# c loaded as eight rows and spread by TensorE, its columns behind x, Sqrt's table ahead of the squares

## The chip, the cores and the metric

The kernel runs on one core of a Trainium2 chip. The metric is the device time of one execution in microseconds, as the median of several runs of the same program. The engines of a core are TensorE (PE; its weight loads are listed as PEld), VectorE (DVE), ScalarE (ACT), GpSimd (POOL) and SyncE (SP), which here issues all DMAs. Each engine takes its instructions in the order in which they were written out, and waits for others by semaphores.

## The reference

One decoder block on x (1024 tokens by 1024 features, float32), steered by one vector c of 1024 numbers:

```python
c_act = silu(c)
cond = c_act @ ada_w + ada_b              # six vectors of 1024: shift1, scale1, gate1, shift2, scale2, gate2
h = rmsnorm(x, norm1_g) * (1 + scale1) + shift1
u, v, val, gate = split(h @ w_in + b_in, 4)
y_a = spatial_gating_mixer(gelu(u), gelu(v), ...)      # chunks of 128 tokens
y_b = conformer_conv_mixer(val, gate, ...)             # causal depthwise conv, width 31
x = x + gate1 * (concat(rmsnorm(y_a), rmsnorm(y_b)) @ w_out)
h2 = rmsnorm(x, norm2_g) * (1 + scale2) + shift2
g, up = split(h2 @ w_ffn_in, 2)
x = x + gate2 * ((silu(g) * up) @ w_ffn_out)
return rmsnorm(x, norm_f_g) * (1 + scale_f) + shift_f  # from c_act @ ada_f_w + ada_f_b
```

The change is about the first two lines and the first rmsnorm: how c and silu(c) reach the engines, and what stands in front of the first product `h @ w_in`.

## The kernel before, in words

**Layout.** Features lie on the 128 partitions, tokens along the free axis. x is held transposed in eight row blocks k of 128 features, and in two halves of 512 tokens, in tiles of two row blocks (`xs[half][i]`). A product in float32 is done as three products of rounded parts, hi x hi, lo x hi and hi x lo (`mm3`, lines 712 to 716; `product`, line 1142): ACT rounds a tile to its hi part, DVE or POOL subtracts to get the lo part.

**The front (lines 586 to 941).** SP issues, in a fixed turn (`in_turn`): the first x tile, c as one row on one partition, the early columns of `colt` (c, the ada biases and norm1's gain as columns), the other x tiles of the first half (the last one in two pieces), then the weights for row block 0: `ada1` (the scale's columns for block 0), one `ada` row block (for the shift) and the first `wk`, then the late columns. TensorE begins with ten matmuls on zeros (`WARM_UP`, line 872). Then it spreads c over all partitions: for each half of c one matmul of a single partition (K = 1) with 512 columns (line 624), and ACT takes Silu of each into `cact` (line 625). Silu of the columns of c is taken apart (line 620). Only then ACT loads the table for Sqrt (line 627).

The first rmsnorm (`first_rstd`, line 845) squares the eight row blocks, some on DVE (`BY_VECTOR`) and some on ACT, into five buffers, sums each over the partitions with four matmuls of 32 columns (line 858), puts matmuls on zeros between them (`IDLE`, `keep_busy`, line 839), takes the square root on ACT (line 862) and the reciprocal on DVE (line 863), and spreads the result over the partitions with matmuls (line 866). The scale of row block 0 comes from `ada1` by matmul (line 891) and a copy (line 894); the other scale and shift columns come from DVE, which multiplies a 128x1024 row block of `ada` by `cact` and sums along the row (line 665). Then per row block k: t = x times the rstd (909 for k = 0, 919 for the others), h = t times scale plus shift in its hi part (922, 924) and its lo part (932, 933), the hi and lo parts of `wk` (697, 698), and 24 matmuls into eight banks (lines 714 to 716).

**After the front.** The u product of the first half (`u_proj`, lo parts of its weights on POOL), the rstd of the second half, the v, value and gate products, the convolution's taps on DVE (line 1071), the mixers, the output projection, then the feed-forward in a Strassen-like form (`product`, line 1147) and the last norm.

**The order.** All engines' orders come from a planner. The program is first written down with its dependencies; `Graph` collects them, `forward` plays the program with a duration for each instruction (`duration`) and for each DMA (`LOAD_WAIT`, `LOAD_RATE`), `backward` gives each step the length of what follows it, and `fix_order` repeats the two `ROUNDS_OF_ORDER` times, with a small random number added to each rank from `SEED`. The order that results is fixed for the whole program on every engine. `in_turn`, `on["V"]` and `on["A"]` are chains that the planner must keep: the loads, DVE's and ACT's steps of the front. Tiles with the same tag share a few buffers (`rt` has two, `cv` and `gn` two PSUM banks each); a new tile waits for the last reader of the old one.

Of the kernel before, what the change touches and what calls it, by code (L numbers as in the profile page):

```python
# [7 lines left out]
F32 = mybir.dt.float32  # L8
F32R = mybir.dt.float32r
BF16 = mybir.dt.bfloat16  # L10
AF = mybir.ActivationFunctionType
ALU = mybir.AluOpType

P = 128
S = 1024
D = 1024
KD = D // P
# [12 lines left out]
N_RAW = 4  # L30
# [2 lines left out]
N_AHEAD = 12  # L33
N_FILL = 8
N_POOL_TAPS = (6, 6)
IDLE = (4, 6, 6, 6, 4)
WARM_UP = 10
BY_VECTOR = (1, 3, 4, 5, 7)
BEFORE_LAST = ((3, 6), (2, 4), (3, 7), (3, 2))
# [5 lines left out]
SHIFT1, SCALE1, GATE1, SHIFT2, SCALE2, GATE2, SHIFTF, SCALEF = range(8)  # L45

_COLS = [
    ("c", 8), ("ada_b", 64), ("norm1_g", 8), ("norm2_g", 8), ("norm_f_g", 8), ("b_in", 16),
    ("a_ln_g", 4), ("a_ln_b", 4), ("b_conv_b", 4), ("b_gn_g", 4), ("b_gn_b", 4),
    ("out_norm_a_g", 4), ("out_norm_b_g", 4), ("b_conv_w", 4 * CW),  # L50
    ("picks", 4), ("low_rows", 1), ("sel_hl", 1),
# [19 lines left out]
SIGNAL = {"PE": 0.043, "DVE": 0.024, "Activation": 0.024, "Pool": 0.068, "SP": 0.05}  # L71
TABLES = ("Sqrt", "Silu", "Sigmoid", "Gelu")
TABLE_LOAD = 1.295
LOAD_WAIT, STORE_WAIT, LOAD_RATE, STORE_RATE = 2.05, 1.29, 350e3, 376e3
LOAD_GAP, STORE_GAP, TURN_GAP = 0.07, 0.24, 0.3
DMA_ISSUE = 0.44
DMA_AHEAD = 0.5
SHORT_ROWS = 1.15
CLOCK_WINDOW = 3.4133
MARGIN = (1.03, 1.1)  # L80
ROUNDS_OF_ORDER, SPREAD, SEED = 4, 0.05, 577509


class Step:
# [452 lines left out]
def block_kernel(ctx: ExitStack, tc: tile.TileContext, xT, c, ada, ada1, cols, vbias, bs, wsp,  # L537
                 wv, wu, wk, wvg, wo, wf, wfo, wfl, cst, out):
    nc = tc.nc
    V, A, G, PE = nc.vector, nc.scalar, nc.gpsimd, nc.tensor  # L540
# [3 lines left out]
    @contextmanager  # L544
    def issue_after(ins):
        n = len(nc.cur_bb.bb.instructions)
        yield
        edges.extend((i.name, ins.name) for i in nc.cur_bb.bb.instructions[n:] if i.engine == ins.engine)

    const = ctx.enter_context(tc.tile_pool(name="const", bufs=1))  # L550
    sb = ctx.enter_context(tc.tile_pool(name="sb", bufs=1))
# [13 lines left out]
    def gn_bank(name):  # L565
        return ps.tile([P, 512], F32, tag="gn", name=name, bufs=2)
# [16 lines left out]
    def hs(half):  # L583
        return slice(half * H, (half + 1) * H)

    c_row = sb.tile([P, D], F32, tag="raw", name="c_row", bufs=N_RAW)
    colt = const.tile([P, NCOL], F32, name="colt")
    xs = [[const.tile([P, 2, H], F32, name=f"x{half}_{i}") for i in range(KD // 2)] for half in range(2)]
    early = _OFF["norm2_g"]
    in_turn = [nc.sync.dma_start(xs[0][0], xT[0, 0]).ins, nc.sync.dma_start(c_row[0:1, :], c).ins,  # L590
               nc.sync.dma_start(colt[:, 0:early], cols[:, 0:early]).ins]
    in_turn += [nc.sync.dma_start(xs[0][i], xT[0, i]).ins for i in range(1, KD // 2 - 1)]
    in_turn += [nc.sync.dma_start(xs[0][KD // 2 - 1][:, a, :], xT[0, KD // 2 - 1, :, a, :]).ins for a in range(2)]

    def x_tile(k, part):
        half = part.start // H
        return xs[half][k // 2][:, k % 2, part.start - half * H:part.stop - half * H]
# [8 lines left out]
    ones = const.tile([P, 1], F32, name="ones")  # L606
    V.memset(ones, 1.0)
    epst = const.tile([P, 1], F32, name="epst")
# [7 lines left out]
    warm = const.tile([P, 1], F32, name="warm")  # L616
    A.activation(warm, epst, AF.Silu)
    cact = const.tile([P, D], F32, name="cact")
    cact_cols = colt[:, 0:KD]
    A.activation(cact_cols, cact_cols, AF.Silu)  # L620
    silu, on = [], dict(V=[], A=[])
    for h in range(2):
        cb = cv_bank(f"c{h}")
        PE.matmul(cb, ones[0:1].broadcast_to([1, P]), c_row[0:1, hs(h)], start=True, stop=True)
        silu.append(A.activation(cact[:, hs(h)], cb, AF.Silu).ins)
    with issue_after(silu[-1]):
        A.activation(warm, epst, AF.Sqrt)


    cond = const.tile([P, 64], F32, name="cond")  # L630
# [214 lines left out]
    def first_rstd():  # L845

        bank = nrm_bank("ssq_n1_0")
        for k in range(KD):
            src = x_tile(k, hs(0))
            t = tmp(f"sq_n1_0_{k}")  # L850
            if k in BY_VECTOR:
                on["V"].append(V.tensor_tensor(t, src, src, op=ALU.mult).ins)
            else:
                on["A"].append(A.activation(t, src, AF.Square).ins)
                if k == 0:
                    on["A"] += silu
            for q in range(4):
                mm = PE.matmul(bank[q * 32:(q + 1) * 32, 0:P], ones.broadcast_to([P, 32]),
                               t[:, q * P:(q + 1) * P], start=k == 0, stop=k == KD - 1).ins
            keep_busy(IDLE[k // 2] if k % 2 else 0, mm)  # L860
        rt = sb.tile([P, P], F32, tag="rt", name="rt_n1_0", bufs=2)
        on["A"].append(A.activation(rt, bank[:, 0:P], AF.Sqrt, bias=epst, scale=1.0 / D).ins)
        last["rstd"] = V.reciprocal(rt, rt).ins
        on["V"].append(last["rstd"])
        for q in range(4):
            mm = PE.matmul(bank[:, q * P:(q + 1) * P], sel_tok[:, q:q + 1].broadcast_to([P, P]),
                           rt, start=True, stop=True).ins
        keep_busy(IDLE[4], mm)
        return bank
# [28 lines left out]
    for k in range(KD):  # L898
# [21 lines left out]
        h = h1[0][k] = act_tile(f"h1_0_{k}", 0)  # L920
# [349 lines left out]
    for p in range(4):  # L1270
        b11, b21, b12, b22 = (ev(f"h2_{n}_{p}") for n in ("11", "21", "12", "22"))
        for kh, (t0, t1) in enumerate(((b11, b12), (b21, b22))):
            k = p + 4 * kh
# [84 lines left out]
    for i, f in enumerate(order):  # L1358
        full7, st, b_bank, s1, up0 = started[f]
        c_bank = cv_bank(f"C_{f}")  # L1360
# [49 lines left out]
    eye = sb.tile([P, P], F32, tag="rt", name="eye", bufs=2)  # L1410
# [72 lines left out]
    for r, pairs in enumerate(ROUNDS):  # L1483
# [10 lines left out]
        base = 0 if last_round else 8 * r  # L1494
# [56 lines left out]
    with issue_after(last_ins):  # L1551
# [6 lines left out]
        for i in (1, 2):  # L1558
            part = pieces[i]
            cols = slice(part.start - H, part.stop - H)  # L1560
# [94 lines left out]
```

## Time and profile before

| | |
|---|---|
| runs | 962.04 us median of 3 (961.86 to 964.15) |
| profiled execution, from its first to its last instruction | 962.3 us |
| TensorE busy | 947.2 us, 98% |
| DVE busy | 859.0 us, 89% |
| ACT busy | 478.8 us, 50% |
| POOL busy | 411.0 us, 43% |
| first product of the front (line 714) | 18.89 us |
| first product of u (line 714, tile pu) | 63.84 us |

The span is the profiled execution's own time: 962.3 us, 0.26 above the median of the runs. In the rows of the timeline the first number is the start in us, the second the time in us, then engine, line, operation, output and inputs, shapes and count; the bracket names the idle time before it and what ended it. "ns" rows by source line give the least, the median and the longest duration, then the first and last start. In the windows view each engine has its busy time in the stretch and the number of instructions, then follow the granted clock of TensorE, the DMA share and GB/s. The chain of waits is followed back from the last instruction.

### The profile page before, as it was taken

The numbers are of one execution on the slowest core, as the hardware profiler recorded it, in microseconds if no ns is written. First come the engines' busy times: TensorE is split into PE (matmuls) and PEld (weight loads), VectorE is DVE, ScalarE is ACT, GpSimd is POOL, SyncE is SP. The second block draws the span as 40 slices with busy tenths as digits, with TensorE's granted clock in tenths as the row PEclk, the third lists the DMA queues.
The fourth block names the chain that finished last, engine by engine and source line by source line (L and its number), as shares of the span: only waits on it lengthen the run. The fifth ranks groups of instructions, "written<-read, shape, count | busy, mean of one in ns | idle before, by whom it ended". The sixth has DMA issues, their size and how long they took to land.

```text
span 962.3 us, 12994 instructions
## 1 busy us (share of the span) xinstructions
PE 947.2 (98%) x4505; PEld 769.7 (80%) x4505; DVE 859.0 (89%) x1234; ACT 478.8 (50%) x771; POOL 411.0 (43%) x253
## 2 busy tenths in 40 slices
PE   8999999999999999999999999999999999999996
PEld 5787787788778778788888888888888888888885
DVE  5978999999999973899999999999978889969956
ACT  4688468863473753564233233332237437227526
POOL 0059997876364313663545534545454200000132
PEclk9999999999999999999999999999999999999998
DMA  8875352353476354844676766667758747414104
GB/s 306 297 278 178 131 176 88 131 182 131 146 267 214 117 175 150 267 167 156 235 250 223 257 225 212 224 231 263 244 173 283 266 164 262 162 33 157 64 0 175
DMA packets 70931, 184.25 MB, mean 191 GB/s; under 512 B 8017, under 2 KB 8529, under 8 KB 70866
## 3 DMA queue, kind: packets, MB, share of 16 engines
q1 hardware_dynamic: 70866, 183.43, 55.1%
q8 instruction: 35, 0.57, 0.3%
q14 instruction: 30, 0.25, 0.1%
HBM read 142.24 MB, written 41.16 MB: 191 GB/s over the span
## 4 chain that ended last, share of the span: by engine, by line
PE 89%; DVE 5%; issue 2%; POOL 2%; ACT 1%; ACTq 0%; POOLq 0%; DVEq 0%
PE B L1147 32%; PE C L1147 18%; PE ah L1147 11%; PE A L1147 4%; PE po L714 3%; PE po L715 3%; PE po L716 3%; PE v L714 2%; PE v L715 2%; PE v L716 2%; PE p L714 1%; PE p L715 1%; PE pu L715 1%; PE p L716 1%; PE pu L716 1%
## 5 line engine op out<-in xcount | busy, mean ns | idle before, releaser
L1147 PE MATMUL B<-h,w_f 128*128 128x512 f32 x816 | 189.7, 389 | 0.0
L1147 PEld LDWEIGHTS B<-h,w_f 128*128 128x128 f32 x816 | 153.1, 188 | 32.1 <-ACT x L1366 0.3
L1071 DVE SCALAR_TENSOR_TENSOR cv<-ypad,colt,cv 128x512 f32<-128x512 f32 x216 | 147.5, 746 | 0.2
L1147 PE MATMUL B<-fa,w_d 128*128 128x512 f32 x528 | 125.1, 389 | 0.0
L1147 PE MATMUL C<-h,w_f 128*128 128x512 f32 x528 | 123.7, 389 | 0.0
L1147 PEld LDWEIGHTS C<-h,w_f 128*128 128x128 f32 x528 | 99.1, 188 | 20.8 <-ACT w_f L1139 0.3
L1147 PEld LDWEIGHTS B<-fa,w_d 128*128 128x128 f32 x528 | 99.1, 188 | 20.6
L1147 PE MATMUL ah<-h,wh_a 128*128 128x512 f32 x320 | 100.4, 391 | 0.5 <-ACT h L731 0.5
L1434 POOL TENSOR_TENSOR sq_nf<-sq_nf,sq_nf 128x512 f32<-128x512 f32 (+1 forms) x15 | 18.4, 1226 | 170.6 <-ACT sq_nf L1428 170.5
L1139 ACT ACTIVATE w_f<-raw_f 128x512 fp32r<-128x512 f32 x68 | 41.9, 628 | 89.9 <-PE C L1147 32.0
L1139 ACT ACTIVATE w_d<-raw_d 128x512 fp32r<-128x512 f32 (+1 forms) x72 | 41.6, 593 | 82.8 <-PE B L1147 30.9
L698 POOL TENSOR_TENSOR wl_a<-raw_a,wh_a 128x1024 fp32r<-128x1024 f32 x20 | 49.0, 2454 | 76.2 <-ACT wh_a L697 76.1
L1147 PEld LDWEIGHTS ah<-h,wh_a 128*128 128x128 f32 x320 | 59.9, 188 | 14.1 <-ACT h L731 0.9
L1140 DVE TENSOR_TENSOR w_f<-raw_f,w_f 128x512 fp32r<-128x512 f32 x68 | 68.3, 1018 | 1.8 <-ACT w_f L1139 1.8
L1147 PE MATMUL C<-fa,w_d 128*128 128x512 f32 (+1 forms) x291 | 64.2, 370 | 0.0
L1147 PE MATMUL ah<-h,wl_a 128*128 128x512 f32 x160 | 62.3, 390 | 0.0
L1394 POOL TENSOR_TENSOR x<-x,u 128x512 f32<-128x512 f32 x22 | 39.4, 1791 | 46.8 <-DVE u L1393 46.8
L1147 PEld LDWEIGHTS C<-fa,w_d 128*128 128x128 f32 x291 | 51.0, 188 | 9.2
L1508 DVE SCALAR_TENSOR_TENSOR x<-B,cond,x 128x512 f32<-128x512 f32 x48 | 35.9, 749 | 19.0 <-PE B L1147 18.2
L1140 DVE TENSOR_TENSOR fa<-a,fa 128x512 fp32r<-128x512 f32 x77 | 50.1, 689 | 2.4 <-ACT fa L1139 2.4
L1391 POOL TENSOR_TENSOR x<-x,up 128x512 f32<-128x512 f32 x20 | 30.9, 1544 | 42.3 <-ACT x L1390 42.2
L1140 DVE TENSOR_TENSOR w_d<-raw_d,w_d 128x512 fp32r<-128x512 f32 (+1 forms) x72 | 48.5, 685 | 0.1
(288 smaller groups left out, 2120.8 us busy)
## 6 DMA issues: line engine op xcount, KB each, us to landing
acts<-x SPq DMA_DIRECT2D x77, 256.0 KB, 2.9
a<-acts SPq DMA_DIRECT2D x77, 256.0 KB, 4.1
raw_f<-wf SPq DMA_DIRECT2D x32, 512.0 KB, 4.1
ada<-ada SPq DMA_DIRECT2D x24, 512.0 KB, 3.3
x<-ada SPq DMA_DIRECT2D x24, 512.0 KB, 4.0
raw_a<-wf SPq DMA_DIRECT2D x20, 512.0 KB, 3.4
ahead<-ahead SPq DMA_DIRECT2D x40, 256.0 KB, 2.4
ypad<-ada SPq DMA_DIRECT2D x16, 512.0 KB, 4.5
```

Source lines behind the costliest of these rows:

```text
L698: lo_eng.tensor_tensor(lo[:, cut], raw[:, cut], hi[:, cut].bitcast(F32), op=ALU.subtract)
L714: PE.matmul(acc, shi, mhi, start=start, stop=False)
L715: PE.matmul(acc, slo, mhi, start=False, stop=False)
L716: PE.matmul(acc, shi, mlo, start=False, stop=stop)
L1071: V.scalar_tensor_tensor(accs[j], src, wc, accs[j], op0=ALU.mult, op1=ALU.add)
L1139: A.activation(dst[:, 0, :], src, AF.Copy)
L1140: lo_eng.tensor_tensor(dst[:, 1, :], src, dst[:, 0, :].bitcast(F32), op=ALU.subtract)
L1147: last_mm = PE.matmul(bank[:, cols], s, m[:, cols], start=first and p == 0 and i == 0, stop=p == n - 1 and i == 2, skip_group_check=True)
L1391: G.tensor_tensor(g0, g0, up0, op=ALU.mult)
L1394: G.tensor_tensor(g1, g1, u2, op=ALU.mult)
L1434: G.tensor_tensor(run, run, t, op=ALU.add)
L1508: V.scalar_tensor_tensor(x_tile(k, part), bank[:, cols], ccol(GATE2, k), x_tile(k, part), op0=ALU.mult, op1=ALU.add)
```

## The change

c is laid out in memory as eight rows of 128 and loaded as a tile of eight partitions behind the first x tile. POOL builds an identity. A matmul of the eight rows with the 8x8 corner of the identity turns them into eight columns in PSUM; ACT takes Silu of these 128x8 numbers. Then ACT loads Sqrt's table. For the broadcast row, each column of silu(c), repeated 128 times as the stationary operand, is multiplied with the identity: eight matmuls of 128x128 into two banks, which ACT copies to `cact`. The columns of `colt` lose c's eight, and the early ones are loaded behind x's first half instead of ahead of its second tile. The matmuls on zeros between the sums go from 22 to 11. The planner's load rate goes from 350 to 400 thousand bytes per us, and its seed is another one, so all orders are made anew. Silu's place in ACT's kept chain behind the first square is gone.

```diff
-IDLE = (4, 6, 6, 6, 4)
+IDLE = (2, 3, 3, 3, 4)
 _COLS = [
-    ("c", 8), ("ada_b", 64), ("norm1_g", 8), ("norm2_g", 8), ("norm_f_g", 8), ("b_in", 16),
+    ("ada_b", 64), ("norm1_g", 8), ("norm2_g", 8), ("norm_f_g", 8), ("b_in", 16),
-LOAD_WAIT, STORE_WAIT, LOAD_RATE, STORE_RATE = 2.05, 1.29, 350e3, 376e3
+LOAD_WAIT, STORE_WAIT, LOAD_RATE, STORE_RATE = 2.05, 1.29, 400e3, 376e3
-ROUNDS_OF_ORDER, SPREAD, SEED = 4, 0.05, 577509
+ROUNDS_OF_ORDER, SPREAD, SEED = 4, 0.05, 17
-    c_row = sb.tile([P, D], F32, tag="raw", name="c_row", bufs=N_RAW)
-    in_turn = [nc.sync.dma_start(xs[0][0], xT[0, 0]).ins, nc.sync.dma_start(c_row[0:1, :], c).ins,
-               nc.sync.dma_start(colt[:, 0:early], cols[:, 0:early]).ins]
+    c_rows = sb.tile([P, P], F32, tag="rt", name="c_rows", bufs=2)[0:KD]
+    in_turn = [nc.sync.dma_start(xs[0][0], xT[0, 0]).ins, nc.sync.dma_start(c_rows, c).ins]
     in_turn += [nc.sync.dma_start(xs[0][i], xT[0, i]).ins for i in range(1, KD // 2 - 1)]
     in_turn += [nc.sync.dma_start(xs[0][KD // 2 - 1][:, a, :], xT[0, KD // 2 - 1, :, a, :]).ins for a in range(2)]
+    in_turn += [nc.sync.dma_start(colt[:, 0:early], cols[:, 0:early]).ins]
     cact = const.tile([P, D], F32, name="cact")
-    cact_cols = colt[:, 0:KD]
-    A.activation(cact_cols, cact_cols, AF.Silu)
-    silu, on = [], dict(V=[], A=[])
+    eye = sb.tile([P, P], F32, tag="rt", name="eye_c", bufs=2)
+    G.memset(eye, 1.0)
+    G.affine_select(out=eye, in_=eye, compare_op=ALU.is_equal, fill=0.0, base=0, pattern=[[1, P]],
+                    channel_multiplier=-1)
+    cact_cols = const.tile([P, KD], F32, name="cact_cols")
+    c_bank = gn_bank("c_cols")[:, 0:KD]
+    PE.matmul(c_bank, c_rows, eye[0:KD, 0:KD], start=True, stop=True)
+    silu_col = A.activation(cact_cols, c_bank, AF.Silu).ins
+    on = dict(V=[], A=[])
+    with issue_after(silu_col):
+        A.activation(warm, epst, AF.Sqrt)
     for h in range(2):
         cb = cv_bank(f"c{h}")
-        PE.matmul(cb, ones[0:1].broadcast_to([1, P]), c_row[0:1, hs(h)], start=True, stop=True)
-        silu.append(A.activation(cact[:, hs(h)], cb, AF.Silu).ins)
-    with issue_after(silu[-1]):
-        A.activation(warm, epst, AF.Sqrt)
+        for i in range(4):
+            PE.matmul(cb[:, i * P:(i + 1) * P], cact_cols[:, 4 * h + i:4 * h + i + 1].broadcast_to([P, P]), eye,
+                      start=True, stop=True)
+        A.activation(cact[:, hs(h)], cb, AF.Copy)
                 on["A"].append(A.activation(t, src, AF.Square).ins)
-                if k == 0:
-                    on["A"] += silu
-        c=arr(c),
+        c=arr(c).reshape(KD, P),
```

More of the change, by code (lines that the diff above doesn't have):

```diff
@@ L1596 @@
     cw = arr(b_conv_w)[0].reshape(CW, 4, P).transpose(2, 1, 0).reshape(P, 4 * CW)
-    colv = dict(c=pcol(arr(c)[0]), ada_b=np.concatenate([pcol(arr(ada_b)[0]), pcol(ada_f_b)], axis=1),
+    colv = dict(ada_b=np.concatenate([pcol(arr(ada_b)[0]), pcol(ada_f_b)], axis=1),
                 norm1_g=pcol(norm1_g), norm2_g=pcol(norm2_g), norm_f_g=pcol(norm_f_g),
```

## The prediction, before the result was known

> **What bounds the kernel now.** I read the page first, then the chain of waits in order of time over the first 60 us, then the timeline by engine, then the landing times of the first loads. All times are from the start of the profiled span.
>
> ```profile
> span 962.3 us, 12994 instructions
> ...
> PE 947.2 (98%) x4505; PEld 769.7 (80%) x4505; DVE 859.0 (89%) x1234; ACT 478.8 (50%) x771; POOL 411.0 (43%) x253
> ```
>
> TensorE is the bound over the whole, 98% busy. So an edit pays if it lets the products begin earlier and if they then run on without a new gap. In the chain, the start looks like this (start, us, what):
>
> ```profile
> 5.31 3.71 PE c L624 x4
> 9.02 1.01 PE ssq_n L858 x16
> ...
> 11.96 0.53 PE p L842 x5
> ...
> 14.31 0.34 PE ssq_n L858 x5
> 14.65 0.02 issue
> 14.67 0.38 ACT rt_n L862
> ...
> 18.75 1.29 DVE wl_k L698 x2
> ```
>
> The broadcast of c (L624, 3.71 us) stands on the chain in front of the sums of squares (L858). They end at 14.65, the square root follows at 14.67, and from 18.75 on the chain is DVE's work on the first row blocks. The products' own rows, from the timeline:
>
> ```profile
> 15.94 1.16 DVE L665 SCALAR_TENSOR_TENSOR ypad<-ypad,cact 128x1024 f32<-128x1024 f32 x1
> 16.54 0.92 PE L866 MATMUL ssq_n<-rt_n,sel_tok 128*128 128x128 f32 x6
> 17.50 0.69 DVE L909 TENSOR_TENSOR t_h<-x,ssq_n 128x512 f32<-128x512 f32 x1 [0.39 <-PE ssq_n L866]
> 18.89 0.97 PE L714 MATMUL p<-h,wh_k 128*128 128x512 f32 x3 [1.11 <-DVE h L922]
> 24.77 1.20 PE L714 MATMUL p<-h,wh_k 128*128 128x512 f32 x4
> 26.54 1.19 PE L715 MATMUL p<-h,wl_k 128*128 128x512 f32 x4 [0.57 <-DVE wl_k L698]
> 63.84 0.39 PE L714 MATMUL pu<-h,wh_u 128*128 128x512 f32 x1
> ```
>
> The first product starts at 18.89, the second row block at 24.77, and the eight blocks end at 63.84. What counts is by how much that 63.84 moves.
>
> **The change part by part.**
>
> *c off the front of TensorE's queue.* Before, the two one-partition matmuls take 5.31 to 9.02, and ACT's squares wait behind the two Silus that follow them. After, only one small matmul (eight columns) and one Silu on 128x8 have to come early; the 16 matmul rows that rebuild the broadcast (8 matmuls, two rows each, as L624 has four rows for two) feed only cact, which nothing reads before the L665 at 15.94.
>
> ```profile
> 5.34 0.21 ACT L620 ACTIVATE colt<-colt 128x8 f32<-128x8 f32 x1 [0.61 <-DMA colt<-cols]
> 15.44 0.28 ACT L894 ACTIVATE scale_rows<-scale_rows 128x128 f32<-128x128 f32 x1 [0.40 <-PE scale_rows L891]
> ```
>
> The small matmul is a new wait: c's eight rows and the identity must be there, and whatever stands behind it in TensorE's queue waits too. When eight rows of 512 bytes land is not in the trace: not before the first x tile ahead of them (4.1), and not after the columns did, the 128 rows that stand one place later now (5.3, where L620 was released). Both are before or at the end of the warm-up matmuls, so it costs nothing. The Silu on eight columns lies between L620's 0.21 and the 128-wide copy from PSUM, 0.28. The sums can then end as early as the last x tile allows. Landings:
>
> ```profile
> L592 SPq DMA_DIRECT2D x<-xT x2: 427/430/432, 2.0 to 2.5; - x2
> DMA to landing us min/median/max: 5.3/5.7/6.1
> L593 SPq DMA_DIRECT2D x<-xT x2: 432/432/432, 3.0 to 3.4; - x2
> DMA to landing us min/median/max: 6.3/6.4/6.5
> L660 SPq DMA_DIRECT2D ypad<-ada x1: 787/787/787, 4.6 to 4.6; - x1
> DMA to landing us min/median/max: 7.9/7.9/7.9
> ```
>
> Second x tile 2.0 + 5.3 = 7.3, third 2.5 + 6.1 = 8.6, last half 3.4 + 6.5 = 9.9; the first ada row block 4.6 + 7.9 = 12.5.
>
> *Columns behind x.* In the windows view the transfers have a hole just where the columns stand in front of the second tile:
>
> ```profile
> 3.50:4.00 0.50, 0.50 (x3) 0.20 (x2) 0.00 (x0) 0.00 (x0) 0.00 (x0) 1.00 0.55 125
> 4.00:4.50 0.50, 0.50 (x3) 0.15 (x1) 0.40 (x1) 0.40 (x1) 0.00 (x0) 1.00 0.61 163
> 6.00:10.00 4.00, 4.00 (x21) 1.30 (x19) 1.64 (x3) 1.54 (x3) 0.00 (x0) 1.00 1.01 392
> ```
>
> (The last two columns are the DMA share and GB/s.) On SP's queue the columns' issue moves past all x issues, so each of these comes one place earlier, at least 0.4 us (2.0 to 2.5 are two issues), and ada's place stays; at most the hole goes and it lands 1.3 after the first, as the third does after the second: 7.3 becomes 5.4 to 6.9. In the two half-microseconds shown (0.45 + 0.39) x 0.5 = 0.4 us of transfer is lost, and 0.4 for the issue: I take 0.9, so the last half tile lands near 9.0 (8.0 to 9.5). Bytes in front of ada stay the same, so its 12.5 stays (10.6 if the hole goes). gain (L881) then waits for columns behind x; it is first needed by the scale column at 16.7, so that costs nothing unless it is queued on DVE ahead of the last square, and then about 1 us.
>
> *The sums.* Square 0.69 (the DVE row below, which also shows the first x tile in at 4.1), then one k of L858. The chain has 16 rows in 1.01 us, and 64 rows make eight k's, so 0.5 each: 9.0 + 0.7 + 0.5 = 10.2, about 10.4 at the square root in place of 14.67. That asks TensorE to have caught up. From the end of the warm-up (5.31) it has: c columns 0.3 (estimate: two rows of the size of L858's or a bit more), sums 8 x 0.43 (16 rows, 0.85 without the gap that follows) = 3.4, c rows 16 x 0.23 = 3.7 (L624's 3.71 is for four rows of 512 columns; these have 128), the 11 idle matmuls that stay beside the sums, at the chain's 0.53 for five, 1.2. In all 8.6 us at the pace of that time, to 13.9. But the pace doubles on the way:
>
> ```profile
> 4.10 0.69 DVE L852 TENSOR_TENSOR sq_n<-x 128x512 f32<-128x512 f32 x1 [2.21 <-DMA x<-xT]
> L858 PE MATMUL ssq_n<-sq_n,ones x64: 272/421/423, 8.9 to 14.3; 128*32 128x128 f32 x64
> ```
>
> L858's 421 ns fall to 272 at the end, about 14, that is 5 us after the matmuls with all 128 partitions began at 8.95. After, they begin at 5.3 with the c rows and the sums: full pace from about 10.4. Then 5.1 us of the 8.6 are done cold and the other 3.5 take 1.75: 12.1. If the order puts the sums ahead of most c rows, 10.4 holds; if behind all, 12.1. Neither is in the trace; I take the middle, 11.3, so the square root comes 3.4 us earlier.
>
> *What comes after.* From 14.67 to the first t_h at 17.50 is 2.83, to the first product 4.22: t_h at 14.1, product at 15.5. The other branch, the shift, needs ada (12.5), L665 and cact: L665 goes from 15.94 to 12.5, again 3.4. Both branches give 3.4, and DVE's chain from there on has the same instructions. So 63.84 becomes 60.4.
>
> *What is hidden.* ACT's rows:
>
> ```profile
> 7.35 0.60 ACT L625 ACTIVATE cact<-c 128x512 f32<-128x512 f32 x1 [1.80 <-PE c L624]
> 10.19 1.28 ACT L627 ACT_TABLE_LOAD   x1
> ```
>
> Sqrt's table (1.28) moves to about 5 to 6.5, where ACT waited 1.80 for L624; the next square cannot start before the second x tile at 5.4 to 6.9. The identity is built on POOL, which is idle then; the one affine_select in the trace takes 2.09 for eight times as many columns, so it is ready by about 3.5, ahead of x at 4.1. The two 0.60 Silus become two Copies of the same size. Two of the "rt" buffers are taken: the copy of the scale rows must wait for the last c row matmul, before 12.1 at the latest, while its data (ada1) lands at 11.2. The banks of c0, c1 and the c columns are needed again only by the first products, at 15.5. Eleven idle matmuls fewer free 1.2 us, counted above.
>
> *The new order.* Load rate and seed draw every engine's order afresh. What it can touch beyond the front is small, since products run back to back:
>
> ```profile
> PE pu L715 <- POOL wl_u L698: 1.3, 1, 1.3
> ...
> PE gn L1122 <- DVE late L649: 0.5, 1, 0.5
> ```
>
> These are the two waits of TensorE behind the front that an order can make or take away, 1.8 together; I take 0 for the new draw, and 1.5 either way, somewhat less than their sum.
>
> **Sum.** 962.3 (span) - 3.4 = 958.9; the runs' median of 962.04 lies 0.26 below the span, hence **958.6**. A measurement here tells no change from a change within 0.3%, 2.9 us; the line is at 959.15.
>
> **The rivals.**
>
> *A better front (957.0).* The hole goes, TensorE is warm in time, and DVE's early work is ordered better: the second block at 24.77 then waits less for wl_k (0.57 at 26.54 and the gap before it). Square root at 10.4 is 4.3 us, with 0.7 more from that block: 5.0. For it speaks that the load rate used for planning (350, then 400) comes nearer to the 392 GB/s above; against it that ada's landing may not move.
>
> *c rows ahead of the sums, all cold (961.2).* The change then does not do what it says: 13.9 in place of 14.67, a gain of 0.8. For it: 16 rows x 0.23 are as long as the L624 they replace. Against: the sums lead to everything, and the queue has pauses while x lands.
>
> *The clock falls back (960.3).* With fewer idle matmuls, a shorter stretch of sums and a wait for ada, the stretch before the first product may be too quiet.
>
> ```profile
> 17.47:20.89 3.42, 2.31 (x13) 1.75 (x14) 3.29 (x6) 2.21 (x6) 0.00 (x0) 1.00 0.91 351
> 952.70:956.13 3.43, 1.63 (x12) 1.35 (x12) 2.93 (x9) 3.15 (x10) 0.00 (x0) 1.00 0.74 274
> 956.13:962.30 6.17, 0.00 (x0) 0.00 (x0) 2.53 (x7) 3.16 (x8) 0.00 (x0) 0.50 0.63 231
> ```
>
> A stretch of 3.43 us with 1.63 busy is followed by a granted clock of 0.50; one with 2.31 kept 1.00. After the sums there remain the scale rows (16 rows, two k's of sums at the doubled pace, 0.4), L866 (eight rows at the 0.15 of the row above, 1.2) and four idle matmuls, 0.2, in 4 us: near that limit. One such stretch of 3.4 us at half speed costs 1.7: 958.6 + 1.7. The Trainium skill (TensorE: Matmul & The Clock Gate, Part 1: The HAM clock gate) has the array return to half clock after an idle window of some 3.4 us; here 1.63 us busy in one was already too little, so the trace is stricter than that sentence.
>
> *POOL in front of the u products (965.4), slower.* After the front TensorE takes wl_u from POOL, whose queue is full there:
>
> ```profile
> L698 POOL TENSOR_TENSOR wl_u<-raw_u,wh_u x4: 2407/3363/3395, 56.4 to 78.2; 128x1024 fp32r<-128x1024 f32 x4
> 80.56 2.09 POOL L808 TENSOR_SCALAR_AFFINE_SELECT wt<-wt 128x1024 f32<-128x1024 f32 x1
> 70.15 1.29 POOL L1066 TENSOR_TENSOR s<-s,cp 128x512 f32<-128x512 f32 x1
> ```
>
> If POOL does not move up with the front (it follows the second half of x), the 3.4 are waited away there; if the new order also puts the affine_select and one more add ahead of the third wl_u, 2.09 + 1.29 = 3.4 are added: 962.0 + 3.4. It decides from the point where that wl_u ends later than it does now. Against: ACT's squares that feed POOL wait for the front's own end, so they move along.
>
> **How the numbers follow.** Forecast 0.50, better front 0.14, c rows ahead 0.15, clock 0.13, POOL 0.08. The forecast's own range is 957 to 960.3; of its 0.50, 0.35 lies under 959.15. With the better front's 0.14 and a little of the clock's: faster 0.52, within 0.3% 0.38, slower 0.10. The range goes from the better front less a lucky draw (957.0 - 1.5) to the c rows ahead with a bad draw (961.2 + 1.8).
>
> **What would show it.** Right: the second x tile lands under 7, the square root stands between 10.4 and 12.1, L665 starts near 12.5, the first product near 15.5, the u products near 60.4, at a granted clock of 1.00, and from there each stage keeps its distance. Wrong: matmuls of c between the sums up to 13 us; first products at twice the 389 ns pace; a wait on wl_u of 4 us or more; or a front 3.4 us shorter with an end that has not moved, which would put the loss in the order further on.

## The result, and the profile after

The changed kernel takes 967.14 us (median of 4, 964.49 to 968.09) against 962.0; the ratio is 1.0047, with an interval of 1.003 to 1.0064. A second timing gave 966.76 and 1.0041 (1.0026 to 1.0056). The forecast was 958.6; the kernel became slower instead. (One execution each of before, `e_body_only` and `e_cols_first`, at 1358 to 3608 us, stands far outside all others and is left out of every median here.)

The front nevertheless looks as the prediction had it. Rows of after's timeline (start, us, engine, line, what):

```profile
4.36 0.35 PE L625 MATMUL c_cols<-eye_c,c_rows 8*128 8x8 f32 x2
5.12 1.28 ACT L629 ACT_TABLE_LOAD   x1
5.42 1.60 PE L633 MATMUL c<-eye_c,cact_cols 128*128 128x128 f32 x12
6.36 0.69 DVE L860 TENSOR_TENSOR sq_n<-x 128x512 f32<-128x512 f32 x1 [1.27 <-DMA x<-xT]
10.89 0.37 ACT L868 ACTIVATE rt_n<-ssq_n,epst 128x128 f32<-128x128 f32 x1 [0.69 <-PE ssq_n L864]
12.16 1.16 DVE L673 SCALAR_TENSOR_TENSOR ypad<-ypad,cact 128x1024 f32<-128x1024 f32 x1
15.20 1.16 PE L722 MATMUL p<-h,wh_k 128*128 128x512 f32 x4 [1.20 <-DVE h L928]
59.36 0.39 PE L722 MATMUL pu<-h,wh_u 128*128 128x512 f32 x1
```

The square root stands at 10.89 (14.67 before), the first product at 15.20 (18.89), the first u product at 59.36 (63.84). Not all of this distance is the edit's: TensorE has its full clock from 4.10 us on in this execution, in before's from 14.06 on, and what that is worth is worked out under "The base of the sum" below. The 4.5 us at the first u product are gone at the end: the span is 962.7 us, against 962.3 before.

That execution took 964.49, the fastest of its four. The second profiled execution of after, `a1_after`, has a span of 965.5. TensorE's longest waits behind 20 us in it (us in total, times, longest; an eighth has 0.4):

```profile
PE ssq_nf L1458 <- DVE rt_nf L1456: 1.6, 1, 1.6
PE po L722 <- ACT y_b L1035: 1.6, 1, 1.6
PE ssq_n L777 <- DVE rt_n L771: 0.8, 1, 0.8
PE ah L1153 <- DVE ypad L798: 0.7, 1, 0.7
PE gn L1128 <- DVE gd L657: 0.5, 1, 0.5
PE ssq_a L777 <- DVE rt_a L771: 0.5, 1, 0.5
PE ssq_nf L1426 <- POOL sq_nf L1440: 0.4, 1, 0.4
```

None of these names a weight's low part. Five are waits for the sums and reciprocals of norms, the other two for y_b and ypad, tiles of the convolution branch, and they lie all over the kernel. And at one of them, in this execution, the granted clock falls (stretch, its length, busy time of PE, PEld, DVE, ACT, POOL, granted clock, DMA share, GB/s):

```profile
343.70:347.11 3.41, 1.68 (x7) 0.86 (x5) 2.64 (x6) 0.48 (x1) 0.00 (x0) 1.00 0.57 189
347.11:350.52 3.41, 3.21 (x8) 2.54 (x9) 3.31 (x7) 2.04 (x4) 0.00 (x0) 0.50 0.00 0
```

### The profile page after: what moved, and what is told of

It is laid out like the page before. It is cut to its first block, busy times and chain, and to the rows that moved or that the text cites. A ratio compares the mean times of both kernels' runs of the same rounds, so it can differ in the third digit from the quotient of the medians.

```text
span 962.7 us, 12991 instructions
## 1 busy us (share of the span) xinstructions
PE 945.4 (98%) x4507; PEld 768.1 (80%) x4508; DVE 866.5 (90%) x1234; ACT 478.4 (50%) x771; POOL 408.8 (42%) x255
## 4 chain that ended last, share of the span: by engine, by line
PE 84%; DVE 8%; DMA 4%; ACT 2%; POOL 1%; issue 1%; SPq 0%; DVEq 0%; ACTq 0%; POOLq 0%
PE B L1153 32%; PE C L1153 19%; PE ah L1153 11%; PE A L1153 4%; DVE cv L1077 3%; PE po L722 3%; PE po L723 3%; PE po L724 3%; PE p L724 2%; PE p L722 2%; PE p L723 2%; DVE ada L673 1%; DMA ada<-ada 1%; DMA ypad<-ada 1%; PE pm L1020 1%
## 5 line engine op out<-in xcount | busy, mean ns | idle before, releaser
L1146 DVE TENSOR_TENSOR w_f<-raw_f,w_f 128x512 fp32r<-128x512 f32 x68 | 57.9, 860 | 0.7 <-ACT w_f L1145 0.6
L1145 ACT ACTIVATE fa<-a 128x512 fp32r<-128x512 f32 x77 | 46.3, 627 | 6.4 <-DMA a<-acts 3.3
```

The costliest lines, as they stand in the source:

```text
L1145: A.activation(dst[:, 0, :], src, AF.Copy)
L1146: lo_eng.tensor_tensor(dst[:, 1, :], src, dst[:, 0, :].bitcast(F32), op=ALU.subtract)
```

## The experiments

### The same two kernels again, and the clock of the front

`a0_before` is the kernel before, `a1_after` the one after, both unchanged.

> The kernel before once more, for the span and granted clock of each of its executions. The changed kernel's profiled span is 962.7 us and its time 964.49, 1.8 more; most of its other executions have spans of 965.3 at a mean clock of 0.995 in place of 0.997. Clock theory (in most executions of the changed kernel a stretch of 3.4 us in the front runs at half clock, 1.7 us lost by the clock itself and 2.6 in all): here nearly all spans are alike, about 960 to 962, at 0.997. Order theory (the new order behind the front loses what the front gains, the clock does not matter): the clock varies here as it does in the changed kernel. Both: ratio 1.000.

> The changed kernel once more, beside the kernel before. Clock theory: most executions at 965 us of span and 0.995, and if the profiled one is among them its trace shows a granted clock of 0.5 for one stretch of 3.4 us between 10 and 20 us; the first products run there at twice their pace. Order theory: a trace like the first one, first product near 15.2 at full clock, the lead over the kernel before 3 to 4 us up to about 120 us and gone by 160; ratio 1.005 with either.

Measured: 963.23 (ratio 1.000, 0.999 to 1.001) and 966.76. The loss repeats, and the mean clocks of before's own executions vary as after's do (0.994 to 0.997). The front of both profiled executions of after has the full clock from 5.8 us on at the latest; a1_after's half clock came at 347 us, where I had not looked, and the first execution has none before the kernel's end. `e_fill` makes the front busy on purpose: 18 matmuls on zeros ahead of the first product, everything else in the order of after.

```diff
+FILL = 18
...
         keep_busy(IDLE[4], mm)
...
+        keep_busy(FILL, mm)
```

> The changed kernel with 18 more idle matmuls of 128 columns in the gap before the first product (1 us of a gap of 1.2), put in after the planner has made its orders, so that nothing else moves. Clock theory: no stretch at half clock, all spans near 962.7 at 0.997, 2.5 us faster than the changed kernel (ratio to the kernel before 1.0025). Order theory: as the changed kernel, ratio 1.005; if the fill delays the first product, up to 1 us slower.

Measured: 966.12 (965.08 to 970.64), ratio 1.0043 (1.003 to 1.0056). No effect. The rival "the clock falls back in the front" is refuted for this kernel; after's own windows say the same, the stretch in which the products begin has 2.55 us busy and the full clock behind it:

```profile
14.34:17.75 3.41, 2.55 (x11) 2.18 (x12) 3.26 (x7) 1.88 (x4) 0.00 (x0) 1.00 1.01 402
17.75:21.16 3.41, 3.16 (x14) 2.29 (x14) 3.41 (x6) 2.47 (x5) 0.00 (x0) 1.00 1.03 410
```

### The new front with the old order behind it, and the reverse

`e_front_only` is after, but on each engine only the steps that the planner ends ahead of 64 us keep the new order; the rest follow in before's order, which is written into the kernel as a list.

```diff
+JOIN = 64.0
...
+        first = [s for s in order[e] if done[s.n] < JOIN]
...
+        rest = [g.steps[n - 1 - i] for i in ends if n - 1 - i not in kept]
+        order[e] = first + rest
```

> The changed kernel up to 64 us of its plan, and behind that each engine's order of the kernel before. Order theory: the lead of 3 to 4 us at the end of the front is kept to the end, 4 to 5 us less than the changed kernel: span 959 where the clock holds, ratio 0.997 to 1.000. Clock theory alone: the order does not matter, ratio 1.005 as the changed kernel. Both: 962 to 963 in executions with the half-clock stretch, 959 to 960 in those without.

Measured: **958.99** (958.55 to 960.33), ratio 0.9964 (0.995 to 0.9977): faster than both kernels. Its waits behind 20 us are fewer and shorter:

```profile
PE ssq_nf L1601 <- POOL sq_nf L1615: 1.0, 1, 1.0
PE ssq_nf L1633 <- DVE rt_nf L1631: 1.0, 1, 1.0
PE gn L1303 <- DVE late L832: 0.5, 1, 0.5
PE ah L1328 <- ACT h L914: 0.5, 1, 0.5
PE p L899 <- DVE h L1114: 0.2, 1, 0.2
```

These are 3.2 us where a1_after's seven rows make 6.1. With the old order behind it the changed kernel takes 3.1 us less than before (962.12, timed beside it), and the new order behind 64 us costs 966.76 - 958.99 = 7.8. Not all of this is itemised: the two profiled executions are 8.4 us apart in span, of which the waits above make 3.3 (with a1_after's eighth), the half clock about 1.7 (half of 3.41) and the front 0.6 (first u product at 60.52 against 59.92); the other 2.8 stand in no row shown here. Two more joins ask where: `e_join_250` keeps the new order up to 250 us of plan (JOIN = 250), and `e_body_only` has before's front and after's order behind 64 us.

> After with its new order up to 250 us of plan, and from there each engine's order of before. The lags against before showed two places where the front's gain is lost: 120 to 160 us (about 3 us) and 333 to 347 us (about 2 us, and 1.7 more by the half clock). Theory, the two places are independent: only the second is mended, so 966.8 - 3.7 = 963.1, range 962.2 to 964, and the full clock at 347 us. Rival 1, the loss lies all in the second place and the first is caught up later: 959 to 960. Rival 2, the late place follows from what came earlier (work left over on DVE and ACT): it comes back elsewhere, 965 to 967.

> The front of before (its first 64 us of plan), and behind it the new order of after on every engine: the mirror of the kernel with the new front and the old order, which took 958.99. Theory, the new order behind the front costs by itself what it cost there (966.76 - 958.99 = 7.8 us, whatever front stands ahead of it): 962.1 + 7.8 = 969.9, and not under 966. Rival 1, the new order only costs because it meets a front that is 3.1 us shorter (transfers, POOL's squares and the front no longer fit each other): then with the old front it costs little, 962 to 964. Rival 2, the price is half and half: about 966. The half clock of one stretch of 3.4 us near 347 to 354 us should be there again by the theory, after a stretch with about 1.7 us busy.

Measured: e_join_250 962.42 (961.4 to 963.57), as the theory had it: 4.3 us of the loss lie behind 250 us, 3.4 ahead of it. e_body_only 976.17 (974.03 to 976.36), far over the 969.9 of the theory: put behind another front, this order has a long wait at a place where a1_after waits 0.8 us,

```profile
84.30 2.08 PE L944 MATMUL ssq_n<-rt_n,sel_tok 128*128 128x128 f32 x8 [5.76 <-DVE rt_n L938]
```

and half clock in two places, behind that wait and at 356 us. A price of the order alone can't be read from it: what an order costs depends on what it was drawn for.

### c's row and the columns, one at a time

Both start from e_front_only. `e_cols_first` loads the early columns ahead of x's second tile, as before. `e_c_row` leaves the columns behind x; beside the eight rows it loads c as one row and spreads that with the two one-partition matmuls, their Silus, and Sqrt's table behind them.

```diff
     in_turn = [nc.sync.dma_start(xs[0][0], xT[0, 0]).ins, nc.sync.dma_start(c_rows, c).ins]
+    in_turn += [nc.sync.dma_start(colt[:, 0:early], cols[:, 0:early]).ins]
...
-    in_turn += [nc.sync.dma_start(colt[:, 0:early], cols[:, 0:early]).ins]
```

```diff
-            PE.matmul(cb[:, i * P:(i + 1) * P], cact_cols[:, 4 * h + i:4 * h + i + 1].broadcast_to([P, P]), eye,
-                      start=True, stop=True)
-        A.activation(cact[:, hs(h)], cb, AF.Copy)
+        PE.matmul(cb, ones[0:1].broadcast_to([1, P]), c_row[0:1, hs(h)], start=True, stop=True)
+        silu.append(A.activation(cact[:, hs(h)], cb, AF.Silu).ins)
```

> The new front with the old order behind it (958.99), but the early columns are loaded ahead of x's second tile, as in before. By my step for the columns (0.9 us for the landings of x's first half, on the chain to the square root), this gives 959.0 + 0.9 = 959.9, the square root at about 11.8 in place of 10.9. Rival 1, TensorE's sums and not x's landing set the square root: 959.0 as it was. Rival 2, the columns' place costs more than their transfer (the hole in the transfers): 1.9, so 960.9.

> The new front with the old order behind it (958.99), but c is also loaded as one row and spread as in before: two matmuls of one partition, Silu of each 512 columns on ACT behind the first square, and Sqrt's table after them. The eight rows stay for the columns of silu(c) alone. By my steps c's spread is the larger part of the front's 3.4 us (2.5 of it, the columns' 0.9 being the rest): 959.0 + 2.5 = 961.5, the square root at about 13.4. Rival 1, the fewer idle matmuls and the columns gave it all: 959.0. Rival 2, ACT's path (Silus, then 1.28 us of table, then squares) is what binds, and all of the gain is lost: 962.1, square root at 14.3 or later.

Measured: 961.68 (959.41 to 965.05) and 962.48 (960.17 to 963.32). The first number misleads: six executions lie at 959.4 to 961.7 and five at 962.9 to 965.1, and the profiled one, 962.93, is of the slower five. In e_cols_first the front is as quick as in e_front_only, whose square root stands at 11.53 (its row is below):

```profile
6.96 0.69 DVE L1035 TENSOR_TENSOR sq_n<-x 128x512 f32<-128x512 f32 x1 [1.94 <-DMA x<-xT]
...
11.32 0.37 ACT L1043 ACTIVATE rt_n<-ssq_n,epst 128x128 f32<-128x128 f32 x1 [0.68 <-PE ssq_n L1039]
```

The columns' place cost nothing there. The time went at 62 us, since the edit had the planner draw the first 64 us anew as well (view of TensorE's waits, 20 to 120 us; half clock follows from 63.00 to 66.41):

```profile
PE pu L897 <- ACT sg L971: 2.5, 1, 2.5
```

e_c_row has the same flaw, and one more. In its profiled execution the spread takes 3.78 us again and the square root is at 14.65, but the full clock came only at 14.18 us there, and at 4.79 in e_front_only's. Beside the new front's profiles with a late clock (square root at 13.10 to 13.29) the row costs some 1.4 us. The time, 962.48, fits the case that all of the gain is lost (962.1); how much of it is c's spread and how much the order drawn with it, e_c_row can't tell.

```profile
4.84 3.78 PE L807 MATMUL c<-c_row,ones 1*128 1x512 f32 x4
14.65 0.37 ACT L1045 ACTIVATE rt_n<-ssq_n,epst 128x128 f32<-128x128 f32 x1 [2.16 <-PE ssq_n L1041]
```

### One instruction, and one wait

At 333 us ACT's queue in a1_after has a copy that waits for a product, with Silu's table and Silu of s behind it:

```profile
333.50 0.60 ACT L1168 ACTIVATE ahead<-ah 128x512 f32<-128x512 f32 x1 [3.66 <-PE ah L1153]
334.11 1.28 ACT L1130 ACT_TABLE_LOAD   x1
335.41 1.53 ACT L1130 ACTIVATE s<-s,colt 128x512 f32<-128x512 f32 x2
...
347.31 0.80 PE L722 MATMUL po<-y_b,wh_o 128*128 128x512 f32 x1 [1.57 <-ACT y_b L1035]
```

`e_ahead_late` moves that one copy behind the squares of s; every other queue keeps its order. `e_keep_clock` leaves the wait for y_b and puts seven products, whose result nothing reads, in front of it.

```diff
+    at = next(i for i, s in enumerate(act) if s.writes and s.writes[0].name.startswith("ahead0_11"))
+    to = next(i for i, s in enumerate(act) if s.writes and s.writes[0].name.startswith("sq_b1_3"))
+    act.insert(to, act.pop(at))
```

```diff
+                    for _ in range(FILL):
+                        PE.matmul(last["gn"], unit(ws[0], 0)[0], full(yl[0])[0], start=True, stop=True)
```

> After with one single instruction moved: ACT's copy of the product ahead (L1168 before 334.11 us, which stands 3.66 us waiting in ACT's queue in front of Sigmoid's or Silu's table and Silu of s) goes behind the four instructions that it delays. Theory, this one place in the new order is the later half of the loss: Silu of s starts 2.2 us earlier (333.2 in place of 335.4, when DVE has s), TensorE's waits of 0.36 and 1.57 us for ssq_b and y_b at 345 to 347 go, and with them the half clock of the following 3.4 us (1.7): 966.8 - 3.6 = 963.2, range 962.4 to 964.2, the same as mending the whole order from there on gave (962.4). Rival 1, the wait comes back in another place or on DVE: 965 to 966.8. Rival 2, only the half clock goes: 965.1.

> After with seven extra products ahead of the first output product that waits for y_b (at 345.7 us; their result is overwritten and nothing reads it), all orders otherwise unchanged: the wait of 1.57 us stays, but TensorE is busy in it. Theory, the half clock of 347.1 to 350.5 us follows from the quiet stretch alone (1.68 us busy in 3.41): clock 1.00 there, and 966.8 - 1.7 = 965.1, or 964.5 as in the execution of after that had no such stretch. Rival 1, the clock falls for another reason: 966.8 as it was, 0.50 again. Rival 2, the extra products last longer than the wait and cost what they save: clock 1.00 and 966 to 967.

Measured: e_ahead_late 965.27 (964.02 to 969.87), ratio 1.0027 (1.0016 to 1.0037). In time that is the second rival, "only the half clock goes" (965.1), but the interval still overlaps after's (1.0026 to 1.0056). The profiled execution is the slowest of its eleven, 969.87, 4 us over the next. In it the copy no longer stands in the way, but the wait does not move:

```profile
339.78 2.67 POOL L768 TENSOR_TENSOR sq_b<-sq_b,sq_b 128x512 f32<-128x512 f32 x2 [5.19 <-ACT sq_b L764]
344.75 0.43 PE L771 MATMUL ssq_b<-sq_b,ones 128*32 128x128 f32 x8
...
351.06 0.50 PE L726 MATMUL po<-y_b,wh_o 128*128 128x512 f32 x1 [1.57 <-ACT y_b L1039]
```

POOL ends the sums' last input at 342.45, and the sums (L771) start only at 344.75: now TensorE's own queue holds them, with output products ahead of them, and from them to y_b it is 6.3 us. My theory named the right instruction and missed what is late next. (In this profiled execution the half clock came at 82 us instead, behind a wait of 2.3 us for the reciprocal of the norm, 0.8 in a1_after.) e_keep_clock took 965.74 (ratio 1.004, 1.0023 to 1.0056), which can't be told from after's 966.76. It has the full clock through the place, but that does not show the extra products at work. The same wait of 1.57 us, with nothing in it, passed at full clock in e_fill, whose stretch of 3.41 us began just ahead of it (first row, 1.84 us busy). e_keep_clock's stretch (second row) began there too, and without its seven products it would have had about 3.41 - 1.57 = 1.84 us busy as well:

```profile
345.37:348.78 3.41, 1.84 (x9) 1.46 (x9) 3.23 (x6) 1.89 (x3) 0.00 (x0) 1.00 0.10 42
```

```profile
347.35:350.76 3.41, 3.41 (x16) 2.50 (x15) 3.27 (x6) 1.90 (x3) 0.00 (x0) 1.00 0.06 25
```

Whether this wait brings the half clock depends on where the stretches of 3.41 us begin in that execution; that it costs 1.7 of the loss is not shown.

### Other draws

Is it this draw, or any draw? Eight kernels change only the planner's load rate and seed, one or both:

```diff
-LOAD_WAIT, STORE_WAIT, LOAD_RATE, STORE_RATE = 2.05, 1.29, 400e3, 376e3
+LOAD_WAIT, STORE_WAIT, LOAD_RATE, STORE_RATE = 2.05, 1.29, 350e3, 376e3
-ROUNDS_OF_ORDER, SPREAD, SEED = 4, 0.05, 17
+ROUNDS_OF_ORDER, SPREAD, SEED = 4, 0.05, 577509
```

> After with the planner's load rate and seed of before (350 thousand bytes per us, 577509): all edits of the change but the two that only redraw the order. Theory, the edits are worth the 3.1 us that the new front gave with the old order behind it, and the loss of 7.8 us belongs to the draw of the order: another draw gives another loss or none, 958 to 964, and less than 965 at any rate. Rival 1, the loss belongs to the edits (a front that ends 3 us earlier meets loads, POOL and ACT that have not moved), so every draw has it: 965 to 968. Rival 2, the old rate and seed are just as good here as they are with the old front: 958.5 to 959.5.

> Before with the planner's load rate and seed of after (400 thousand bytes per us, 17): only the draw, none of the edits. Theory, the draw by itself moves the time by several us where I had taken 1.5 either way: outside 960.5 to 963.5, likely slower, 964 to 970, as before's order has been the best of many and a new one is likely to have waits like those of after. Rival, one draw is worth at most 1.5 us, and the loss in after needs the new front: 960.5 to 963.5.

> After with only the seed of before (577509); the load rate stays at 400. If the rate is what counts, this is like after, 965 to 968.5. If each draw stands by itself, anything from 959 to 973 (the draws so far: 959.0, 966.8, 972.1), and I expect it slower than 962. If the seed is what counts, it is near the 972.1 of the old rate with this seed.

> After with only the load rate of before (350); the seed stays at 17. If the old rate is what costs with the new front (972.1 with the old seed), this is 970 to 974. If the seed counts, it is near after's 966.8. If each draw stands by itself, 959 to 973, slower than 962 more likely than not.

> After with another seed (1), rate 400. If the rate sets the loss, 965 to 968.5 as after. If the draws are a lottery, 959 to 973, and the three seeds at this rate lie more than 3 us apart.

> After with another seed (2), rate 400. If the rate sets the loss, 965 to 968.5 as after. If the draws are a lottery, 959 to 973, and the three seeds at this rate lie more than 3 us apart.

> Before with rate 400 and seed 1, none of the edits. If before's own order was an uncommonly good draw, this redraw loses as after's does: 965 to 973, about after's 970.8 plus the front's 3.1 if the same seed gave a like order, which it need not. If redraws only lose behind the new front: 960.5 to 963.5.

> Before with rate 400 and seed 2, none of the edits. If before's own order was an uncommonly good draw: 965 to 973. If redraws only lose behind the new front: 960.5 to 963.5.

| edits of | rate | seed | label | median us | ratio to before |
|---|---|---|---|---|---|
| before | 350 | 577509 | (before) | 962.0 | 1 |
| before | 400 | 17 | d_before_new_draw | 965.86 | 1.0031 (1.0018 to 1.0044) |
| before | 400 | 1 | d_before_seed1 | 965.44 | 1.0029 (1.0012 to 1.0045) |
| before | 400 | 2 | d_before_seed2 | 965.89 | 1.0034 (1.0019 to 1.0049) |
| after | 400 | 17 | a1_after | 966.76 | 1.0041 (1.0026 to 1.0056) |
| after | 350 | 17 | d_rate | 966.04 | 1.0039 (1.0025 to 1.0053) |
| after | 350 | 577509 | d_old_draw | 972.13 | 1.0102 (1.0085 to 1.0118) |
| after | 400 | 577509 | d_seed | 972.86 | 1.0111 (1.0097 to 1.0126) |
| after | 400 | 1 | d_seed1 | 970.81 | 1.0097 (1.0082 to 1.0113) |
| after | 400 | 2 | d_seed2 | 968.75 | 1.0079 (1.006 to 1.0097) |
| after, old order behind 64 us | | | e_front_only | 958.99 | 0.9964 (0.995 to 0.9977) |

The two rates lie 0.7 us apart either time, which the intervals don't tell from nothing; the seed moves the time by up to 6. d_old_draw missed its theory (under 965) and both rivals, and the seeds came out as the lottery had it. All three redraws of before are slower than its own order, by 3.4 to 3.9, so before's order was a good draw and giving it up had a price of its own. Redraws of the changed kernel lose more: 7.1 to 13.9 against e_front_only. At rate 400 three of the four seeds (1, 2 and 577509) share one place: waits of 1.8 to 3.8 us for h that end at 266 to 268 us, with half clock there. Here it is in d_seed (waits of 260 to 280 us, then windows):

```profile
PE ah L1153 <- ACT h L739: 3.8, 1, 3.8
```

```profile
264.97:268.38 3.41, 0.40 (x2) 0.30 (x2) 3.41 (x6) 3.40 (x6) 1.67 (x1) 1.00 0.65 196
268.38:271.80 3.42, 3.42 (x9) 2.31 (x8) 2.80 (x5) 3.42 (x8) 0.00 (x0) 0.50 0.99 333
```

In the redraws of before that wait is 0.4 to 0.6 us and the clock stays. Why the new kernel's orders run into it more often stays open.

## Why the prediction was wrong, by its steps

**The base of the sum.** I wrote that the median lies 0.26 below the span of 962.3. Time and span of one execution are 1.8 us apart: a0_before's profiled one took 964.02 with a span of 962.2, after's 964.49 with 962.7. The page's execution is thus the 964.15 one of the three runs, not the median. It belongs to a group: of the 93 executions of before that were timed beside the other kernels, 60 took 960.81 to 962.45 and 33 took 963.49 to 964.75, with nothing between (of a0_before's own twelve, one lies there, at 963.02). Both profiles of before, the one on whose rows I built and a0_before's, are of the slower group. What differs can be seen in a redraw of before whose front runs the same instructions, if in an order drawn anew; first a0_before, then d_before_seed1:

```profile
5.24 3.78 PE L624 MATMUL c<-c_row,ones 1*128 1x512 f32 x4
14.38 0.37 ACT L862 ACTIVATE rt_n<-ssq_n,epst 128x128 f32<-128x128 f32 x1 [2.18 <-PE ssq_n L858]
18.61 0.95 PE L714 MATMUL p<-h,wh_k 128*128 128x512 f32 x3 [1.12 <-DVE h L922]
63.62 0.39 PE L714 MATMUL pu<-h,wh_u 128*128 128x512 f32 x1
```

```profile
4.45 1.98 PE L624 MATMUL c<-c_row,ones 1*128 1x512 f32 x4
11.69 0.37 ACT L862 ACTIVATE rt_n<-ssq_n,epst 128x128 f32<-128x128 f32 x1 [1.76 <-PE ssq_n L858]
15.69 0.96 PE L714 MATMUL p<-h,wh_k 128*128 128x512 f32 x3 [1.11 <-DVE h L922]
60.58 0.50 PE L714 MATMUL pu<-h,wh_u 128*128 128x512 f32 x1 [0.54 <-ACT sg L788]
```

```profile
4.01:7.43 3.42, 3.42 (x25) 1.15 (x22) 1.55 (x3) 2.40 (x5) 0.00 (x0) 1.00 0.95 332
7.43:10.84 3.41, 3.34 (x47) 2.65 (x47) 1.98 (x3) 2.26 (x4) 0.00 (x0) 0.50 1.04 404
```

Where the clock is full by 4 us, c's spread takes 1.98 in place of 3.78 and the square root stands at 11.69. (The windows view shows 1.00 also ahead of the first record of the clock; in a0_before that record is at 13.48, and the pace of L858, 421 ns, tells of the half clock until then.) All profiles with before's way of spreading c fall into the two kinds: square root at 14.38, 14.65 and 14.67 with the first record at 13.5 to 14.2, or at 11.69, 11.81, 11.86 and 11.96 with it at 4.0 to 5.4. The mean granted clock tells the groups apart in the runs too, the wrong way round because of that missing record: it is 0.997 in a0_before's profiled execution and 0.995 in d_before_seed1's. Of before's executions the slower group has 0.996 or 0.997 (one of the 33 has 0.946), the faster one 0.993 to 0.995, which fits a half stretch on record like that of 7.4 to 10.8. That the faster group is the early clock is inferred from this; no profile of before itself fell into it. The Trainium skill (TensorE: Matmul & The Clock Gate, Part 1: The HAM clock gate) says that the activity window is free-running and the warm-up differs from run to run. The traces agree: the stretches of 3.41 us begin elsewhere in each. Counted back from the first record, the six profiles with a late clock (three with before's way of spreading c, three with the new one) have a boundary between 3.24 and 3.95 us, the fourteen with an early clock between 4.01 and 5.77, so it is not the edit that decides the kind. If the groups are these two kinds, the difference is worth 2.3 us in before (medians 961.78 and 964.04).

**c off the front, 3.4 us.** Between a0_before and e_front_only the first u product moves from 63.62 to 59.92, by 3.7, and the size looks right. But that sets a late clock beside an early one, and is luck. Early beside early, the square root stands between 11.69 and 11.96 with before's front and between 10.89 and 12.18 in ten of the thirteen profiles with the new one, about 0.5 earlier in the middle. Late beside late, it stands between 14.38 and 14.67 with before's front and between 13.10 and 13.29 in the other three (clock full from 10.5 to 10.8), 1.1 to 1.6 earlier. So this term was too large, though it is not what turned the result round. First e_keep_clock, then e_front_only:

```profile
13.29 0.37 ACT L874 ACTIVATE rt_n<-ssq_n,epst 128x128 f32<-128x128 f32 x1 [0.69 <-PE ssq_n L870]
```

```profile
11.53 0.37 ACT L1043 ACTIVATE rt_n<-ssq_n,epst 128x128 f32<-128x128 f32 x1 [0.69 <-DMA raw_k<-wk]
15.85 1.16 PE L897 MATMUL p<-h,wh_k 128*128 128x512 f32 x4 [1.20 <-DVE h L1103]
...
59.92 0.39 PE L897 MATMUL pu<-h,wh_u 128*128 128x512 f32 x1
```

So e_front_only's 3.1 us against the median isn't c's alone: this early-clock execution of it, at 958.77, is 3.0 under even the faster group of before. Before waits 1.3 for POOL's wl_u at the u products; e_front_only has no such wait, and its new order of the first 64 us gives POOL wl_u as its first work (first a0_before, then e_front_only):

```profile
56.01 3.38 POOL L698 TENSOR_TENSOR wl_u<-raw_u,wh_u 128x1024 fp32r<-128x1024 f32 x1
```

```profile
49.00 2.65 POOL L881 TENSOR_TENSOR wl_u<-raw_u,wh_u 128x1024 fp32r<-128x1024 f32 x1 [47.41 <-PE p L898]
```

In an early-clock run of before the products reach that place sooner and should wait longer; no profile shows one. How the 3.1 divide between c and this order was not tried. My rival "POOL in front of the u products" had the place right and the sign wrong.

**Columns behind x, 0.9 of landing.** Not seen. The square of the second x tile starts between 6.36 (after) and 7.98 (a1_after) in the thirteen profiles with the columns behind x, and between 6.35 and 7.54 in the seven with the columns ahead of its second tile (7.33 before). What differs from one execution to the next is larger than what the move brings.

**The sums.** "Full pace from about 10.4" was wrong in ten of thirteen profiles, where the clock was full from 4.0 to 5.8, so that the sums ran at the full pace and the squares, which wait for x, set the square root (in a1_after three squares from 9.27 to 11.40 ahead of it at 12.18). The result, 10.4 to 12.1, came out for another reason. Where the pace did change near 10.4, in the other three, the square root stands at 13.1 to 13.3, a microsecond behind the range.

**What is hidden.** Held: in after the small matmul at 4.36 and the table at 5.12 end before ACT's next square, and L673 stands at 12.16 (12.5 forecast; 13.45 in a1_after).

**The new order, "I take 0 for the new draw, and 1.5 either way".** This is the step that failed. Measured: 7.8 us in after, 3.4 to 3.9 for before alone, up to 13.9 in other draws. I sized it from two waits of before's trace, 1.8 us. But that trace says what this order leaves, not what another brings in: of a1_after's waits those for y_b, rt_n, ypad and rt_a, 3.6 us together, don't stand in before's list of waits at all, and the one for rt_nf at the last norm, which I had left out, grew from 1.0 to 1.6. The middle was wrong too: no redraw came out on the good side of zero.

The sum landed within 0.4 us of e_front_only, but not by its own steps: a base 2.1 too low (962.04 for a profile of 964.15), and a front credited with 3.4 where 5.2 went between two single executions (964.02 to 958.77), the clock's late start and the wait on wl_u among it. That it came so near is luck.

## What to carry to other kernels

An order drawn by a seed is a change with a price of its own; time an edit with the old order held, and take a redraw as a draw whose middle is not zero when the order in hand is a good one. Before a sum is made on a profiled execution, see which group of the runs it is from: its own time is the span and what lies around it, not the median. And set a late clock beside a late one, an early one beside an early one. A wait in a trace bounds what an edit can win there; it does not bound what a new order can lose.

## What the runs showed of the hardware

A stretch of 3.41 us with 1.68 busy (0.40 in d_seed) is followed by one at half the clock, and all clock records ahead of the end lie a multiple of 3.41 apart. In the twenty profiles each of the 27 stretches at full clock with at most 1.76 us busy (18 of them at the kernel's end) was followed by half the clock; with 1.84 or 1.85 us it stayed full five times, and above that it was lost three times, at 2.10, 2.21 and 2.31 us, apart from the case that follows.

With before's front the clock fell after a stretch in which TensorE was busy throughout, 3.42 of 3.42 us, but with c's one-partition matmuls in 1.98 of it (4.01 to 7.43 above; the same in d_before_seed2 and in e_body_only). With 1.67 us of them in a stretch it stayed at 1.00 (d_before_new_draw, 5.39 to 8.80), and so it did with the new front's matmuls of c (after, 4.10 on). That one-partition matmuls count little for the clock fits this; it was not tried alone. It does not explain the late clock: that comes with the new front too, only one stretch earlier, at 10.5 to 10.8 us in place of 13.5 to 14.2.
